# Sixteen experts in pairs: four 32-column tiles of plain fp32 in place of three split passes

## Chip, cores and metric

The kernel runs on one core of one Trainium2 chip. The metric is device time in microseconds (us) of one execution; a kernel's time is the median of its runs. The engines are named as the profile names them: PE (TensorE), PEld (its weight loads), DVE (VectorE), ACT (ScalarE), POOL (GpSimd) and SP (SyncE, which here only issues DMAs).

## What is computed

A chain of two hybrid layers (mixers and a dense FFN) is followed by a second block: an mLSTM and Fourier mixer, then a hierarchical mixture of experts. Both kernels do everything up to the router alike; the change is in the mixture. There are 256 tokens of width 1024, 4 groups of 4 experts, 2 experts chosen per token, both inside the one group that the token picked, and a hidden width of 512 per expert. All weights are fp32.

```python
g_sel = jnp.argmax(g_logits, axis=-1)                       # one group of 4
top_v, top_i = lax.top_k(e_sel, TOP_K)                      # 2 experts inside that group
w_top = jax.nn.softmax(top_v, axis=-1) * p_sel
expert_id = g_sel[..., None] * EXPERTS_PER_GROUP + top_i
combine = jnp.sum(jax.nn.one_hot(expert_id, N_EXPERTS) * w_top[..., None], axis=-2)
for e in range(N_EXPERTS):
    a = jax.nn.silu(h @ lp['w_gate'][e]) * (h @ lp['w_up'][e])
    y = y + combine[..., e, None] * (a @ lp['w_down'][e])
```

The weights of the experts are 16 x 3 x 2 MiB = 96 MiB, and each byte is read once by both kernels.

## The kernel before

**Routing** (`route`, L1211 to L1266). The router's logits stand in PSUM, tokens on partitions. A few dozen small DVE instructions rank them, and each token gets a slot, its rank among the tokens of its *group* (matmuls L1226 and L1228, `slot` L1231). `comb` holds a token's weights for the 16 experts. `over` says whether a group has more than its 128 slots.

**Gather** (`gather`, L1268). A one-hot matrix `oh` (token x slot) is built by DVE, and 32 matmuls (L1281) multiply it with the token matrix to give `xg`, the slots' inputs with the width on partitions. Two groups are gathered at a time, 256 columns per matmul. `h2h` and `h2l` are the high and the low part of the tokens; the matmuls are of type fp32r, which takes fewer bits of an operand than fp32, so a number is kept as a high part and the rest.

**One expert** (`expert_gate`, `expert_up`, `expert_split`, `expert_out`). 128 slots are the columns of the stationary operand. Each weight tile of 1 MiB is loaded into `raw`, then `split` (L189 to L192) makes two fp32r tiles of it: ACT casts to `whi` (L191), DVE subtracts to `wlo` (L192). `mm3` (L241 to L247) then runs three passes, high x high, high x low and low x high, 512 columns each. That makes 24 matmuls for gate, 24 for up and 24 for down, 72 per expert and 1152 for 16 experts. Between up and down stand 4 transposes (L1328). Four experts of a group accumulate in the same two PSUM banks, so the output is moved back to token order once per group (`combine`, 8 matmuls L1354).

**Order.** `moe` (L1361) writes the instructions so that the next expert's gate runs ahead of this expert's transposes, and up ahead of down. Each engine's queue then runs in order.

**Weight buffers.** `raw` (L194) hands out whatever is free: four tiles of a pool from earlier stages, two of `wx`, and at first places that other tensors take later. A load into a buffer waits until DVE has subtracted the last tile in it.

**End** (`finish` L1437, then L1420 and L1421). The result is normalised, added to the input and stored. Every engine then loads `over` (L1420) and branches (L1421) past a body that redoes slots beyond 128; it does not run with these inputs, before or after.

```python
for ps in range(3):                                   # L243, mm3
    for (wh, wl), (xh, xl) in terms:
        w, x = ((wh, xh), (wh, xl), (wl, xh))[ps]
        self.nc.tensor.matmul(out, w, x, ...)         # L247
```

For a later step one place of the first block matters as well: L522 to L529, where attention output is accumulated in fp32 with 64 columns of stationary, a head with an even number into PSUM partitions 0 to 63 and an odd one into 64 to 127. The loop over heads is outside, that over two blocks of keys inside.

Of the kernel before, what the change touches and what calls it, by code (L numbers as in the profile page):

```python
# [17 lines left out]
P = 128  # L18
D = 1024
NEG = -1e30  # L20
SPREAD = (0, 2, 4, 6, 1, 3, 5, 7)
# [121 lines left out]
class Build:  # L143
    def __init__(self, ctx, tc, ins, out, offs, dbg=None):
        self.tc, self.nc, self.ins, self.out, self.dbg = tc, tc.nc, ins, out, dbg or {}
        self.offs, self.at = offs, {}
        pool = lambda name, bufs, **k: ctx.enter_context(tc.tile_pool(name=name, bufs=bufs, **k))
        self.const = pool("const", 1, side="right")
        self.wraw = pool("wraw", 3)
        self.psum = pool("psum", 1, space=bass.MemoryType.PSUM)  # L150
        self.pool = pool
        self.pending = None
        self.wx, self.wy, self.nraw = None, None, 0
# [40 lines left out]
    def raw(self, shape):  # L194
        n, self.nraw = self.nraw, self.nraw + 1
        if self.wx:
            i = n % 10 if n < 20 else (n - 20) % 6
            if i == 8:
                return self.big("raw", shape[1:])
            if i >= 6:  # L200
                return self.act.tile(shape, F32, tag=("xgh", "xgl", None, "yo")[i - 6], name="raw", bufs=1 if i == 9 else 2)
            if i >= 4:
                return self.wx.tile(shape, F32, tag="raw", name="raw")
        else:
            i = n % 4
        if self.wy and i == 3:
            return self.wy.tile(shape, F32, tag="raw", name="raw")
# [1003 lines left out]
    def route(self):  # L1211
# [9 lines left out]
        rank = self.ranks(v[:, 0:2], 2, "g")  # L1221
        asg = tmp.tile([P, 2, 4], FR, tag="asg", name="asg", bufs=1)
        nc.vector.tensor_scalar(asg, rank, 0.0, None, op0=OP.is_equal)
        own = asg.bitcast(F32)
        ps = self.bank()
        nc.tensor.matmul(ps[:, 0:8], self.striu, asg.rearrange("p j g -> p (j g)"), start=True, stop=False,  # L1226
                         skip_group_check=True)
        nc.tensor.matmul(ps[:, 4:8], self.onesr, asg[:, 0], start=False, stop=True, skip_group_check=True)  # L1228
        self.slot = keep.tile([P, 2, 4, 4], F32, tag="slot", name="slot")[:, :, :, 0]
        nc.vector.tensor_scalar(self.slot, own, -1000.0, 1000.0, op0=OP.mult, op1=OP.add)  # L1230
        self.slotted = tt(self.slot, self.slot, ps[:, 0:8].rearrange("p (j g) -> p j g", j=2), op=OP.add)  # L1231
        for j in range(2):
            nc.tensor.matmul(ps[:, 8:12], self.onesr, asg[:, j], start=j == 0, stop=j == 1, skip_group_check=True)
# [7 lines left out]
        rank = self.ranks(ve, 8, "e")  # L1241
# [19 lines left out]
        self.split(comb, *(self.idc[:, :, o:o + 16].rearrange("p j (g i) -> p j g i", g=4) for o in (P, P + 16)))  # L1261
        self.over = keep.tile([P, 5], mybir.dt.int32, tag="over", name="over")
        mxc = small("mxc", 1)
        nc.vector.tensor_reduce(mxc, ps[:, 8:12], AX.X, OP.max)
        nc.vector.tensor_scalar(self.over[:, 0:4], ps[:, 8:12], 128.0, None, op0=OP.is_gt)
        nc.vector.tensor_scalar(self.over[:, 4:5], mxc, 128.0, None, op0=OP.is_gt)  # L1266

    def gather(self, p, slot):  # L1268
        nc = self.nc
        oh = self.act.tile([P, 2, 2, P], FR, tag="oh", name="oh", bufs=2)  # L1270
        for j in range(2):
            nc.vector.tensor_tensor(oh[:, j], self.p("iota")[:, None, :].to_broadcast([P, 2, P]),
                                    slot[:, j, 2 * p:2 * p + 2, None].to_broadcast([P, 2, P]), op=OP.is_equal)
        X = self.hilo("xg", 8, 256, bufs=2)
        yield oh, X
        for q in range(4):
            ps = self.bank()
            for k in range(2):
                f = slice((2 * q + k) * P, (2 * q + k + 1) * P)
                for i, (j, s) in enumerate(((0, 0), (1, 0), (0, 1), (1, 1))):  # L1280
                    nc.tensor.matmul(ps[:, k * 256:(k + 1) * 256], self.H2[s][:, j, f],  # L1281
                                     oh[:, j].rearrange("p n s -> p (n s)"), start=i == 0, stop=i == 3)
            t = self.act.tile([P, 2, 256], F32, tag="xgt", name="xgt", bufs=2)
            for k in range(2):
                m = 2 * q + k
                nc.scalar.activation(t[:, k, :], ps[:, k * 256:(k + 1) * 256], AF.Identity, bias=self.cols[:, 2, m:m + 1],
                                     scale=self.cols[:, 1, m:m + 1])
            self.split(t, X[0][:, 2 * q:2 * q + 2], X[1][:, 2 * q:2 * q + 2])
            yield

    def select(self, g, oh):
        nc = self.nc
        ps = self.bank()
        for j in range(2):
            nc.tensor.matmul(ps[:, j * 160:(j + 1) * 160], oh[:, j, g % 2, :], self.idc[:, j, :], start=True, stop=True)
        v = ps[:, 0:320].rearrange("p (j s) -> p j s", j=2)
        oT = self.act.tile([P, 2, P], FR, tag="oT", name="oT", bufs=2)
        nc.scalar.copy(oT, v[:, :, 0:P])
        cw = self.act.tile([P, 4], F32, tag="cw", name="cw", bufs=2)
        for i in range(4):  # L1300
            e = 4 * g + i
            nc.vector.tensor_reduce(cw[:, i:i + 1], v[:, :, P + e:P + 32:16], AX.XY, OP.add)
        return oT, cw

    def expert_in(self, name, e, X):
        w = self.ins[name][e].rearrange("q p (k c) -> p q k c", k=4)
        n = slice(e // 4 % 2 * P, (e // 4 % 2 + 1) * P)
# [7 lines left out]
    def expert_gate(self, e, X):  # L1315
        ga = self.tmp.tile([P, 512], F32, tag="ga", name="ga")
        self.nc.scalar.activation(ga, self.expert_in("w_gate_2", e, X), AF.Silu)
        return ga

    def expert_up(self, e, X, ga, cw):  # L1320
        self.nc.vector.scalar_tensor_tensor(ga, self.expert_in("w_up_2", e, X), cw[:, e % 4:e % 4 + 1], ga,
                                            op0=OP.mult, op1=OP.mult)

    def expert_split(self, ga):
        nc = self.nc
        ps = self.bank()
        for m in range(4):
            nc.tensor.transpose(ps[:, m * P:(m + 1) * P], ga[:, m * P:(m + 1) * P], self.c("ident"))  # L1328
        A = self.hilo("ah", 4, P, bufs=2)
        self.split(ps.rearrange("p (m s) -> p m s", m=4), *A)  # L1330
        return A

    def expert_out(self, e, A, acc):
        w = self.ins["w_down_2"][e].rearrange("q p (k c) -> p q k c", k=2)
        for q in range(2):
            W = self.weights(w[:, q], 2, 1024, -2 if e else -4)
            for hf in range(2):
                self.mm3(acc[hf], [((A[0][:, 2 * q + k, :], A[1][:, 2 * q + k, :]),
# [236 lines left out]
```

## Time and profile before

| | us |
|---|---|
| runs | 1139.29, 1140.35, 1140.89 (median 1140.35) |
| profiled execution | 1136.58 |
| its span in the profile | 1134.7 |
| PE busy | 1073.8 (95%) |
| DVE busy | 894.6 (79%) |
| ACT busy | 643.5 (57%) |
| POOL busy | 130.2 (11%) |
| read from memory | 246.01 MB, 218 GB/s over the span |

The span runs from the first to the last instruction of the profiled execution; 1.9 us lie around it. Times of a row are from the start of the span. Matmuls overlap: a row of a group gives for each matmul the time from its start to its modelled end (some 0.4 us for 512 columns), while the next one starts earlier, and the chain of waits shows the step from one start to the next. The granted clock is 1.00 where PE has its full 2.4 GHz and 0.50 at 1.2 GHz.

### The profile page before, as it was taken

What the parts mean: (1) busy time and instruction counts of PE and PEld (TensorE: products, weight loads), DVE (VectorE), ACT (ScalarE), POOL (GpSimd) and SP (SyncE); (2) the same over time, 40 slices, a digit from 0 to 9 for tenths busy, and PEclk for the clock granted to TensorE, in tenths of its full rate; (3) what the DMA queues carried; (4) which work ended last, traced back from release to release, by engine and by line L of the source; (5) the groups of instructions that cost most, each with busy time, mean ns of one, the idle gap of its engine ahead of it and who ended that gap; (6) DMA issues with size and microseconds to landing.
All of it is one profiled execution on the core that took longest, in us unless ns stands there. A gap on an engine that the chain in (4) does not pass through costs nothing.

```text
span 1134.7 us, 18470 instructions
## 1 busy us (share of the span) xinstructions
PE 1073.8 (95%) x7384; PEld 974.0 (86%) x7384; DVE 894.6 (79%) x1448; ACT 643.5 (57%) x937; POOL 130.2 (11%) x139
## 2 busy tenths in 40 slices
PE   7997999999999989899999989899899999999995
PEld 6896999999998978899999988877788888878783
DVE  6897678888777977856877778775599888998976
ACT  5635554344455364635554345743687778777763
POOL 3190010000020930310000022000000000000001
PEclk9998999999999989989999999899899999999998
DMA  8634347776754244555667750320678689989871
GB/s 283 232 112 167 131 152 275 247 254 242 268 187 149 103 158 154 213 189 210 236 237 283 294 207 24 144 75 12 265 274 339 259 323 344 350 345 371 302 299 41
DMA packets 41390, 248.34 MB, mean 219 GB/s; under 512 B 4560, under 2 KB 6992, under 8 KB 15312
## 3 DMA queue, kind: packets, MB, share of 16 engines
q1 hardware_dynamic: 41296, 247.08, 59.0%
q8 instruction: 60, 0.98, 0.3%
q14 instruction: 34, 0.28, 0.1%
HBM read 246.01 MB, written 1.05 MB: 218 GB/s over the span
## 4 chain that ended last, share of the span: by engine, by line
PE 46%; DVE 4%; ACT 2%; issue 1%; POOL 1%; POOLq 0%; DVEq 0%; ACTq 0%
PE mm L247 23%; PE acc L247 14%; DVE wlo L192 1%; ACT whi L191 1%; PE mm L1354 1%; PE mm L1281 1%; PE mm L733 1%; PE mm L1328 1%; PE acc L922 1%; PE mm L805 0%; POOL ssq L285 0%; PE mm L1063 0%; PE mm L1064 0%; DVE Mt L757 0%; PE mm L1129 0%
## 5 line engine op out<-in xcount | busy, mean ns | idle before, releaser
L191 ACT CAST whi<-raw 128x1024 fp32r<-128x1024 f32 (+2 forms) x375 | 406.0, 1124 | 262.2 <-PE mm L247 124.7
L192 DVE TENSOR_TENSOR wlo<-raw,whi 128x1024 fp32r<-128x1024 f32 (+2 forms) x375 | 484.2, 1326 | 80.5 <-ACT whi L191 79.4
L247 PE MATMUL mm<-hfh,whi 128*128 128x256 f32 x672 | 91.5, 278 | 0.1
L247 PE MATMUL mm<-hfl,whi 128*128 128x256 f32 x672 | 90.4, 277 | 0.0
L247 PE MATMUL mm<-hfh,wlo 128*128 128x256 f32 x672 | 90.1, 277 | 0.0
L285 POOL TENSOR_TENSOR ssq<-ssq,sqt 128x256 f32<-128x256 f32 x40 | 38.2, 957 | 430.1 <-ACT sqt L277 428.8
L247 PEld LDWEIGHTS mm<-hfh,whi 128*128 128x128 f32 x672 | 83.2, 188 | 0.4 <-ACT whi L191 0.4
L247 PEld LDWEIGHTS mm<-hfl,whi 128*128 128x128 f32 x672 | 82.7, 188 | 0.0
L247 PEld LDWEIGHTS mm<-hfh,wlo 128*128 128x128 f32 x672 | 82.7, 188 | 0.0
L247 PE MATMUL acc<-ffh,whi 128*128 128x256 f32 x352 | 72.0, 285 | 0.0
L247 PE MATMUL mm<-whi,xgh 128*128 128x512 f32 x256 | 71.7, 399 | 0.4 <-ACT xgh L191 0.3
L247 PE MATMUL acc<-ffh,wlo 128*128 128x256 f32 x352 | 71.0, 283 | 0.0
L247 PE MATMUL acc<-ffl,whi 128*128 128x256 f32 x352 | 70.7, 282 | 0.0
L247 PE MATMUL mm<-wlo,xgh 128*128 128x512 f32 x256 | 70.4, 395 | 0.0
L247 PE MATMUL mm<-whi,xgl 128*128 128x512 f32 x256 | 70.0, 395 | 0.0
L696 DVE CUSTOM_DVE_ANT_0 araw<-araw,arow 128x1024 f32<-128x1024 f32 x48 | 58.5, 1231 | 0.0
L247 PEld LDWEIGHTS mm<-wlo,xgh 128*128 128x128 f32 x256 | 47.9, 187 | 11.9 <-DVE wlo L192 0.3
L247 PEld LDWEIGHTS mm<-whi,xgl 128*128 128x128 f32 x256 | 48.0, 187 | 11.7
L247 PEld LDWEIGHTS mm<-whi,xgh 128*128 128x128 f32 x256 | 46.8, 188 | 11.7 <-ACT xgh L191 1.2
L247 PEld LDWEIGHTS acc<-ffh,whi 128*128 128x128 f32 x352 | 55.0, 192 | 0.2
L247 PEld LDWEIGHTS acc<-ffl,whi 128*128 128x128 f32 x352 | 54.8, 191 | 0.0
L247 PEld LDWEIGHTS acc<-ffh,wlo 128*128 128x128 f32 x352 | 54.8, 191 | 0.0
(489 smaller groups left out, 2034.8 us busy)
## 6 DMA issues: line engine op xcount, KB each, us to landing
raw<-in_w_gate_dram SPq DMA_DIRECT2D x54, 1024.0 KB, 5.4
raw<-in_w_up_dram SPq DMA_DIRECT2D x54, 1024.0 KB, 5.2
raw<-in_w_down_dram SPq DMA_DIRECT2D x54, 1024.0 KB, 4.9
raw<-in_w_in_dram SPq DMA_DIRECT2D x29, 1024.0 KB, 4.9
araw<-in_w_adaT_dram SPq DMA_DIRECT2D x48, 512.0 KB, 5.0
raw<-in_w_out_dram SPq DMA_DIRECT2D x12, 1024.0 KB, 4.8
x<-in_xT_dram SPq DMA_DIRECT2D x4, 256.0 KB, 5.5
raw<-in_w_in_dram SPq DMA_DIRECT2D x4, 256.0 KB, 5.6
```

Source lines behind the costliest of these rows:

```text
L191: nc.scalar.copy(hi, src)
L192: nc.vector.tensor_tensor(lo, src, hi.bitcast(F32), op=OP.subtract)
L247: self.nc.tensor.matmul(out, w, x, start=start and i == 0, stop=stop and i == n - 1, **kw)
L285: nc.gpsimd.tensor_tensor(self.ssq, self.ssq, sq, op=OP.add)
L696: nc.vector.tensor_tensor_reduce(out, raw, rows[n], 1.0, 0.0, OP.mult, OP.add, self.mod[:, t, n:n + 1])
L733: nc.tensor.matmul(ps[0:100, :], self.weff[:, (c + 4) % 8, :], src, start=c == 0, stop=c == 7)
L922: nc.tensor.matmul(psx[m][:, 0:258], a, b[:, k, :], start=k == 0 and i == 0, stop=k == 7 and i == 2)
L1281: nc.tensor.matmul(ps[:, k * 256:(k + 1) * 256], self.H2[s][:, j, f], oh[:, j].rearrange("p n s -> p (n s)"), start=i == 0, stop=i == 3)
L1328: nc.tensor.transpose(ps[:, m * P:(m + 1) * P], ga[:, m * P:(m + 1) * P], self.c("ident"))
L1354: nc.tensor.matmul(ps, oT[:, j, :], Y[:, s, hf, :], start=s == 0, stop=s == 1)
```

## The change

Experts p and p+8 form a pair, and there are 8 pairs. A pair has 128 slots too, but they belong to experts now: four columns of 32 slots. Column 1 is expert p+8, columns 2 and 3 are expert p, and column 0 is assigned by count: to p+8 if it has more than 32 tokens, else to p. `side[p]`, an integer made by DVE in `route`, is loaded into a PE register (`sides`, L1341), and the weight tile holds both experts' weights next to each other, so the register picks the half that the matmul of column 0 reads.

For each weight slice `quads` (L1344 to L1347) issues four matmuls, each with 32 columns of stationary, writing to its own 32 PSUM partitions, and reading 512 columns of its own expert's weights. They are plain fp32 on the weights as loaded: no `split`, no high and low. Per pair gate has 32 matmuls in 8 quads, up the same, and down, in two halves, the same; 192 quads in all.

What follows from that: a gather for every pair (L1312; 32 matmuls of 128 columns, moved out of PSUM by ACT L1319 and DVE L1316 in turn), a select and 4 transposes (L1370) for every pair, and a combine (8 matmuls, L1391) for every pair. The host lays the weights out anew, 4 tiles of 1 MiB for each of gate, up and down of a pair. The weight buffers are a ring of 16 tiles (3 of the old pool, 13 new ones). Routing gets longer (`room`, `past`, `put`, `full`, `late`, `side`, `pairs`), and three rounds for slots beyond the columns stand at the end instead of one, each behind a load and a branch (L1445, L1446).

```diff
+RING = (6, 7, 11, 8, 1, 4, 2, 5, 0, 3, 9, 10, 12)
     def raw(self, shape):
         n, self.nraw = self.nraw, self.nraw + 1
-        if self.wx:
-            i = n % 10 if n < 20 else (n - 20) % 6
...
+        if self.ring:
+            i = n % (3 + len(self.ring))
+            if i >= 3:
+                return self.act.tile(shape, F32, tag=f"ring{self.ring[i - 3]}", name="raw")
...
-        rank = self.ranks(v[:, 0:2], 2, "g")
+        rank = self.ranks(v, 10, "r")
...
+        nc.vector.tensor_scalar(self.side, ps[:, 40:48], 32.0, None, op0=OP.is_gt)
...
+    def pair(self, name, p, q):
+        w = self.raw([P, 2, 2, 512])
+        self.nc.sync.dma_start(w, self.ins[name][p, q].rearrange("p (e k c) -> p e k c", e=2, k=2))
+        return w
+
+    def sides(self, p):
+        v = self.nc.values_load(self.side[0:1, p:p + 1], engines=(mybir.EngineType.PE,), min_val=0, max_val=1)
+        return [bass.ds(v, 1), slice(1, 2), slice(0, 1), slice(0, 1)]
+
+    def quads(self, out, x, w, side, start, stop):
+        for t in range(4):
+            r = slice(32 * t, 32 * t + 32)
+            self.nc.tensor.matmul(out[r], x[:, r], w[:, side[t]].rearrange("p e c -> p (e c)"), start=start, stop=stop)
+
+    def pair_in(self, name, p, X, side):
         ps = self.bank()
-        for q in range(2):
-            W = self.weights(w[:, q], 4, 512, -2 if e else -4, self.held if q else ())
-            self.mm3(ps, [((X[0][:, 4 * q + k, n], X[1][:, 4 * q + k, n]), (W[0][:, k, :], W[1][:, k, :]))
-                          for k in range(4)], start=q == 0, stop=q == 1)
+        for q in range(4):
+            w = self.pair(name, p, q)
+            for k in range(2):
+                self.quads(ps, X[:, 2 * q + k], w[:, :, k, :], side, q == 0 and k == 0, q == 3 and k == 1)
         return ps
...
+        for r in range(3):
+            rv = nc.values_load(self.over[0:1, 3, r:r + 1])
+            with self.tc.If(rv > 0):
```

**PE, an expert and a pair.** In the rows, `whi` and `wlo` are the two parts of a weight tile, `xgh` and `xgl` those of the gathered slots, `ga` the gated product, `raw` a weight tile as loaded, `xg` the gathered slots in fp32. Before, the end of a gate, the transposes of the expert ahead, and an up:

```order
L247 MATMUL mm<-whi,xgh 128x512 x4
L247 MATMUL mm<-wlo,xgh 128x512 x4
L247 MATMUL mm<-whi,xgl 128x512 x4
L1328 MATMUL mm<-cst_160,ga 128x128 x4
L247 MATMUL mm<-whi,xgh 128x512 x4
L247 MATMUL mm<-wlo,xgh 128x512 x4
L247 MATMUL mm<-whi,xgl 128x512 x4
```

Now, the first gate, from the gather's last matmuls on:

```order
L1312 MATMUL mm<-oh,h2l 128x128 x3
L1347 ISA
L1347 MATMUL mm<-raw,xg 32x512
L1312 MATMUL mm<-oh,h2h 128x128 x2
L1312 MATMUL mm<-oh,h2l 128x128 x2
L1347 MATMUL mm<-raw,xg 32x512 x3
L1347 ISA
L1347 MATMUL mm<-raw,xg 32x512 x4
L1347 ISA
L1347 MATMUL mm<-raw,xg 32x512 x4
```

Each quad stands behind one register instruction (ISA), and is a row of its own. The gather's last four matmuls stand inside the first quad, behind its first matmul; such broken quads come 8 times. In all the queue changes between 32-column matmuls and matmuls of the full width 115 times.

**SP, the loads around the start of the mixture.** `in_w_out_dram` is the last weight of the mixer. Before:

```order
L229 DMA raw<-in_w_out_dram 128x2048 x4
L234 DMA raw<-in_w_up_dram 128x2048
L234 DMA raw<-in_w_gate_dram 128x2048 x2
L234 DMA raw<-in_w_up_dram 128x2048
L234 DMA raw<-in_w_gate_dram 128x2048 x3
L234 DMA raw<-in_w_down_dram 128x2048 x2
L234 DMA raw<-in_w_up_dram 128x2048 x2
```

Now:

```order
L1337 DMA raw<-in_w_gate_dram 128x2048 x4
L1337 DMA raw<-in_w_up_dram 128x2048 x4
L1337 DMA raw<-in_w_gate_dram 128x2048 x4
L1337 DMA raw<-in_w_up_dram 128x2048 x4
L1337 DMA raw<-in_w_down_dram 128x2048 x4
```

The loads now come in the order in which PE reads them, the first 16 into 16 buffers; load 17 waits until PE has read load 1.

**DVE, routing.** `slot` is what the one-hot matrix `oh` needs, `h2l` is the low part of the tokens. Before, from `slot` to `h2l`:

```order
L1231 TENSOR_TENSOR slot<-slot,mm 128x8
L1244 TENSOR_SCALAR top<-rank 128x32
L1245 TENSOR_SCALAR second<-rank 128x32
L1272 TENSOR_TENSOR oh<-cst_5015,slot 128x256
...
L1272 TENSOR_TENSOR oh<-cst_5015,slot 128x256
L1161 SCALAR_TENSOR_TENSOR h2l<-x_8185,rs_8845,h2h 128x512
```

Now:

```order
L1246 SCALAR_TENSOR_TENSOR put<-put,sel 128x32
L1285 TENSOR_TENSOR room<-mm,room 128x16
L1247 SCALAR_TENSOR_TENSOR slot<-put 128x16
L1272 TENSOR_TENSOR w_8947<-w_8947,psel 128x8
L1286 TENSOR_TENSOR most<-room 128x8
L1295 TENSOR_TENSOR oh<-cst_5015,slot 128x256
...
L1281 TENSOR_TENSOR pairs<-comb 128x16
L1156 SCALAR_TENSOR_TENSOR h2l<-x_8185,rs_8845,h2h 128x512 x2
```

Between the matmuls that count the tokens and `slot` stand some 20 small instructions now, 2 before; between the first `oh` and `h2l` 13 in place of 9.

## Rows read from the trace of the kernel before

**Rows 1.** Page, part 1: each engine's busy time, share of the span, instructions.
```profile
PE 1073.8 (95%) x7384; PEld 974.0 (86%) x7384; DVE 894.6 (79%) x1448; ACT 643.5 (57%) x937; POOL 130.2 (11%) x139
```
**Rows 2.** Chain of waits that ended last, in the mixture: start us, us, what.
```profile
830.19 2.61 PE mm L247 x10
...
847.35 0.44 PE mm L1328 x4
847.79 5.59 PE mm L247 x24
...
1109.36 10.07 PE acc L247 x42
1119.43 1.43 PE mm L1354 x4
```
**Rows 3.** Window table: stretch, busy us of each engine, granted clock, DMA share, GB/s.
```profile
814.00:824.00 10.00, 7.33 (x31) 6.73 (x32) 6.28 (x36) 7.28 (x18) 0.98 (x1) 0.50 0.80 318
830.00:1104.00 274.00, 273.74 (x1229) 220.83 (x1230) 243.87 (x259) 209.17 (x250) 0.00 (x0) 1.00 0.85 326
804.00:812.00 8.00, 8.00 (x43) 6.37 (x41) 3.83 (x7) 4.39 (x13) 1.10 (x2) 1.00 0.96 389
1020.00:1040.00 20.00, 20.00 (x89) 16.13 (x89) 17.82 (x17) 14.93 (x17) 0.00 (x0) 1.00 0.95 365
```
**Rows 4.** Timeline of PE around plain fp32 matmuls of 512 columns (L892).
```profile
696.35 1.02 PE L892 MATMUL mm<-par,cst 128*128 128x512 f32 x2
697.21 0.38 PE L805 MATMUL mm<-vt,kw 128*128 128x129 f32 x2
```
**Rows 5.** Timeline of PE around two places with 64-column fp32 matmuls.
```profile
424.68 0.50 PE L247 MATMUL mm<-xnh,wlo 128*128 128x256 f32 x2
425.11 1.09 PE L527 MATMUL acc<-pT,vt 128*64 128x128 f32 x14
426.13 0.39 PE L247 MATMUL mm<-xnh,wlo 128*128 128x256 f32 x1
...
85.67 0.66 PE L538 MATMUL mm<-wsT,ones 128*64 128x128 f32 x8
```
**Rows 6.** Durations of such a line (ns, min/median/max).
```profile
L538 PE MATMUL mm<-wsT,ones x16: 272/273/323, 85.7 to 402.9; 128*64 128x128 f32 x16
```
**Rows 7.** Chain of waits: small matmuls of the mixture.
```profile
905.27 0.94 PE mm L1281 x8
...
1082.64 1.79 PE mm L1176 x16
```
**Rows 8.** Line L1420, the load of the test's value into a register, by engine's queue.
```profile
L1420 DVEq TENSOR_LOAD <-over x1: 753/753/753, 1127.9 to 1127.9; - x1
L1420 SPq TENSOR_LOAD <-over x1: 482/482/482, 1129.7 to 1129.7; - x1
```
**Rows 9.** Line L1421, the branch, and what stands behind it (EVENT_SEMAPHORE), by queue.
```profile
L1421 SPq EVENT_SEMAPHORE  x9: 17/17/17, 1132.7 to 1133.3; - x9
...
L1421 DVEq EVENT_SEMAPHORE  x2: 21/21/21, 1132.3 to 1132.4; - x2
...
L1421 SPq COMPARE_BRANCH  x1: 45/45/45, 1130.2 to 1130.2; - x1
```
**Rows 10.** Timeline of DVE in routing.
```profile
821.14 0.28 DVE L1205 TENSOR_TENSOR gt<-lt 128x128 f32<-128x128 f32 x1
821.34 0.18 DVE L1208 TENSOR_REDUCE rank<-gt 128x8 f32<-128x32 f32 x1
821.44 0.28 DVE L1206 TENSOR_TENSOR ge<-ge,cst 128x128 f32<-128x128 f32 x1
...
822.54 0.17 DVE L1231 TENSOR_TENSOR slot<-slot,mm 128x8 f32<-128x8 f32 x1
...
824.99 0.75 DVE L1161 SCALAR_TENSOR_TENSOR h2l<-x,rs,h2h 128x512 fp32r<-128x512 f32 x1
```
**Rows 11.** Timeline of SP: three of the mixture's first loads, four stand ahead of them.
```profile
802.87 1.28 SPq L234 DMA_DIRECT2D raw<-in_w_gate_dram  x3
```

More of the change, by code (lines that the diff above doesn't have):

```diff
@@ new lines, in route @@
+        self.slot = keep.tile([P, 2, 8], F32, tag="slot", name="slot")
+        put = small("put", 2, 2, 8)
+        for h, b in enumerate((64.0, 32.0)):
+            nc.vector.tensor_scalar(put[:, :, h], before[:, :, h], b, -2 * b, op0=OP.is_ge, op1=OP.mult)
+            nc.vector.scalar_tensor_tensor(put[:, :, h], before[:, :, h], b, put[:, :, h], op0=OP.add, op1=OP.add)
+        full = small("full", 2, 2, 8)
+        nc.vector.tensor_scalar(full, past, 0.0, 1000.0, op0=OP.is_ge, op1=OP.mult)
@@ L1266, in route @@
-        nc.vector.tensor_scalar(self.over[:, 4:5], mxc, 128.0, None, op0=OP.is_gt)
-    def gather(self, p, slot):
-        nc = self.nc
[L1270 to L1276, printed above, removed]
+        pairs = small("pairs", 2, 2, 4)
@@ new lines, in route @@
+        tt(pairs, comb[:, :, 0:2], comb[:, :, 2:4], op=OP.add)
+        self.split(pairs, *(self.idc[:, :, o:o + 8].rearrange("p j (g i) -> p j g i", g=2) for o in (P, P + 8)))
+        self.over = keep.tile([P, 4, 8], mybir.dt.int32, tag="over", name="over")
+        most, big = small("most", 8), small("big", 1)
+        tt(room, ps[:, 32:48].rearrange("p (h e) -> p h e", h=2), room, op=OP.subtract)
+        tt(most, room[:, 0], room[:, 1], op=OP.max)
+        nc.vector.tensor_reduce(big, most, AX.X, OP.max)
@@ L1283, in gather @@
[L1283 to L1291, printed above, removed]
+                    nc.tensor.matmul(ps[:, k * P:(k + 1) * P], self.H2[s][:, j, m * P:(m + 1) * P],
+                                     oh[:, j], start=i == 0, stop=i == 3)
@@ L1342, in group_out, with pair_out @@
-    def group_out(self, acc):
+        nc.scalar.copy(A, ps.rearrange("p (m s) -> p m s", m=4))
+        return A
+    def pair_out(self, p, A, side):
         Y = self.act.tile([P, 2, 2, 512], FR, tag="yo", name="yo")
         for hf in range(2):
-            self.split(acc[hf], Y[:, 0, hf, :], Y[:, 1, hf, :])
+            acc = self.bank("acc", 4)
+            for q in range(2):
+                w = self.pair("w_down_2", p, 2 * hf + q)
+                for k in range(2):
+                    self.quads(acc, A[:, 2 * q + k], w[:, :, k, :], side, q == 0 and k == 0, q == 1 and k == 1)
+            self.split(acc, Y[:, 0, hf, :], Y[:, 1, hf, :])
@@ new lines, in moe @@
+        for r in range(3):
+            rv = nc.values_load(self.over[0:1, 3, r:r + 1])
+            with self.tc.If(rv > 0):
+                late = self.tmp.tile([P, 2, 2, 8], F32, tag="sl2", name="sl2", bufs=1)
+                nc.vector.tensor_scalar(late, self.late, -64.0 * r, None, op0=OP.add)
+                for p in range(8):
+                    rp = nc.values_load(self.over[0:1, r, p:p + 1])
+                    with self.tc.If(rp > 0):
+                        oh = self.hot(p, late)
+                        X = self.gather(oh)
+                        oT, cw = self.select(p, oh)
+                        ga = self.pair_gate(p, X, side)
+                        self.pair_up(p, X, side, ga, cw)
+                        self.combine(y, oT, self.pair_out(p, self.pair_turn(ga), side))
+                self.finish(x2, y, yg, g2)
@@ L1517, in run @@
         phb.close()
+        phw.close()
         pha.close()
         if stop != "mix":
-            self.wx, self.nraw = pool(ph3, "wx", 2), 0
+            self.ring, self.wy, self.nraw = RING, None, 0
             self.act = pool(ph3, "act3")
+            for i in range(len(RING)):
+                self.act.tile([P, 2048], F32, tag=f"ring{i}", name="place")
             self.tmp = pool(ph3, "tmp3", 2)
```

222 lines of the change are left out of this document (103 added, 119 removed).

## The prediction, made before the changed kernel was timed

> **What bounds the kernel now.** I read the page's first part, then the chain of waits, then a window table of the mixture. Part 1 gives PE 95% of the span and DVE 79% [rows 1], an average over stages. The chain shows the stage that is changed: from 830.19 to 1119.43 us it is PE alone, gate and up, transposes, down, one after another [rows 2]; in the window from 830 to 1104 PE is busy 273.74 of 274.00 us at granted clock 1.00, with DVE at 243.87 and the DMA share 0.85 [rows 3]. So in these 289.2 us PE sets the time. A group of 24 matmuls takes 5.59 us, 0.233 us each, and 1152 x 0.233 = 268.8; transposes, gathers, combines and selects make up the rest. The reader should see that splitting, however busy DVE is, is covered: to delete it saves nothing by itself.
>
> The sum goes against the profiled execution, 1136.58 us (span 1134.7, 1.9 around it), which is 3.8 us under the median of the runs.
>
> **PE: 1152 fp32r matmuls go, 192 quads come.** A plain fp32 matmul has two records, one per pass; two records of 512 columns start at 696.35 and the next work at 697.21, so it takes 0.86 us, 0.43 a pass [rows 4]. The price of a quad hangs on whether its four matmuls run at once. The nearest rows have two column tiles of 64: 8 records in 0.66 us and 14 in 1.09 us [rows 5], where one record lasts 0.272 [rows 6]. The 14 are seven calls, and by the loops their order is one head's call in the lower tile, two in the upper, two lower, two upper: 6 records for the lower tile and 8 for the upper. Eight steps of 0.109 us plus the first step's 0.05 and the last record's tail give 7 x 0.109 + 0.05 + 0.27 = 1.08: the time of the longer tile alone. So the two tiles run side by side, though a tile's own records stand four in a row. I take the same for four tiles: 0.86 us per quad. The ends are 0.86 and, if none run together, 3.44; what I hold possible in between are the rivals below.
>
> The Trainium skill's page "TensorE: Matmul & The Clock Gate", section "Part 3: Packing small matmuls — row/col tiling", says that matmuls start and end strictly in program order. Here that rule would make a quad 1.72 us and the kernel some 165 us longer than my sum; the 14 records speak against it, and it is rival D.
>
> The terms of the new stretch:
> - 192 quads x 0.86 = 165.1.
> - 8 broken quads: a lone first matmul costs a full 0.86 and the other three another, so 8 x 0.86 = 6.9.
> - Gathers of 7 more pairs, 7 x 32 matmuls of 128 columns. Matmuls of the full width with few columns take 0.11 (4 in 0.44 [rows 2], 16 in 1.79 [rows 7]); half of a 256-column one (8 in 0.94 [rows 7]) would be 0.06. I take 0.11, as a weight load comes with each: 24.6.
> - Combines 64 x 0.233 = 14.9, transposes 32 x 0.11 = 3.5, selects 16 x 0.11 = 1.8, the row of L1176 1.8 as before.
> - Changes of tile shape. Around the 14 records [rows 5] I find four delays. The full-width matmul ahead starts at 424.90 (two with a record of 0.28 fill 0.50) and needs 0.12, yet the first tile starts at 425.11: 0.09. The first step is 0.05 longer. The last start is 425.11 + 0.05 + 7 x 0.109 = 425.92, yet the next matmul starts at 426.13, not 0.11 later: 0.10. That one lasts 0.39 in place of 0.28: 0.11. Together 0.35 us a round trip. 115 changes are 57 round trips: 19.9. The low end is nothing, if the next weights load meanwhile.
> - 8 loads of `side` into a register: 0.48 us each, as SP's queue shows one [rows 8], plus two register instructions, at most 4.6, at least nothing, as PE has queued work; I take 2.4. The 192 register instructions ahead of the quads: the nearest row is a branch of 45 ns on a queue [rows 9], so at most 9; the queue runs ahead by 0.86 us per quad, so nothing.
> - The clock is at 0.50 while PE waits for the routing [rows 3]: 1.5 for the first quads, between 0 and 3.
>
> The sum is 242.4 us against 289.2: **46.8 less**. Per pair that is 30.3 us.
>
> **What leaves the other engines.** The 192 casts and subtractions go; nothing waited for them, so no gain. ACT and DVE take on the evacuation of seven gathers, 8 small instructions per pair on two engines that lose 24 large ones each: covered by 30 us of PE per pair.
>
> **The start is later.** `slot` is ready at 822.54 now [rows 10]. The ranks of ten rows rather than two cost 5 x 0.1 more (128 elements take a step of 0.20, 32 elements 0.10 [rows 10]); some 20 small instructions at about 0.10 stand ahead of `slot`, of which two stood there before. Against that, the half of the gather's evacuation on DVE and the split of `xg` that is gone bring the first quad forward. The low part `h2l`, now behind 13 small instructions, comes at 827 to 828 instead of 824 to 825.7 and the gather waits for it. I put the first quad at 831.9 where the first matmul stood at 830.19: **+1.7**, between -1 and +4.
>
> **The tail is longer.** Two more tests stand on each queue, one after the other. SP's load takes 0.48, its branch 0.05, and from the branch at 1130.2 to what stands behind it at 1132.7 it is 2.5; DVE's load starts at 1127.9 and takes 0.75, and what stands behind its branch is at 1132.3, together 4.4 [rows 8, 9]. Two more are 2 x 3.0 to 2 x 4.4: I take **+7**, between 0 (if the later jumps are cheap) and 9.
>
> **The loads.** 96 MiB as 96 loads of 1 MiB, now in the order of use. A busy stretch had 389 GB/s at share 0.96 (2.70 us per MiB), the best 20 us in the mixture 365 (2.87) [rows 3]. Before, the first seven loads were out by 804.2 [rows 11]; the first of them wait for the same buffers now, so I count seven landed at 812. Nine more at 2.70 fill the ring of 16 at 836, when PE has begun to free it; the 80 left take 216 us, to 1052, while PE works to 832 + 242 = 1074. So the stream is covered by 22 us; it would bind from 3.0 us per MiB on (350 GB/s). What is late next, if PE were faster, is this stream.
>
> Together: -46.8 + 1.7 + 7 = -38.1, so 1098.5 for the profiled execution and, 3.8 higher, **1102 us** on the scale of the medians.
>
> **Rivals.**
> - **B, cheaper PE.** Gathers at 0.06 (-11) and tile changes hidden (-20) leave 211 us of PE, to 1043; then the loads bind, at 2.70 us to 1052 and 3 for the last work, so 19 us are gained on 1074: 1083. Where they don't bind it is all 31: 1071. For it: queues on PE run ahead of the array. Against it: the rows of 0.11 and of the tile changes, measured here.
> - **E, the loads bind.** The mean of the mixture, 326 GB/s [rows 3], is 3.22 us per MiB: 80 x 3.22 = 257, to 1093, and 3 for the last: +22, 1124. For it: that mean. Against it: those loads waited for DVE to free buffers.
> - **C, four tiles overlap in part.** Four streams of columns have to be read where the rows show two. By the rows a quad then lies between 0.86 and D's 1.72; a quarter of the way is 1.08, and 192 x 0.22 = +42 gives 1144, about as before. Against it: with two tiles the rows show no loss at all. The Trainium skill's table in the same section has three column tiles at 2.38 times the speed of one; an efficiency of 0.79 would, as an estimate from that page, make a quad 1.09 us and the time about the same 1144; no run here shows it yet.
> - **D, the order of the matmuls decides.** If a matmul cannot start before the one ahead of it in the queue, the second pass of column 0 holds column 1, and so on; each quad then takes four steps of 0.43, 1.72 us: +165, **1267 us, slower**. The same price follows if the matmul with the register's address does not run beside the others. It decides from a quad of 1.06 us on (38.1 / 192 = 0.20 above 0.86). For it: no row here has a register as an address, nor four tiles. Against it: the 14 records.
>
> **How the numbers follow.** A measurement of this kernel can tell about 0.2%, 2.3 us, from no change. The forecast, with E inside it, 1085 to 1128: 0.67, and 1102 is its likeliest value. B, 1067 to 1085: 0.12. C, 1128 to 1155: 0.09, half of it still faster. D, around 1267: 0.12. The range 1067 to 1149 takes in the forecast, B and most of C and leaves D out, which is a little over one in ten. Faster: 0.67 + 0.12 + 0.04 = 0.83; within 0.2%: 0.02; slower: 0.15.
>
> **What would show it.** The line of `quads`: four starts within some ns and 0.86 us between quads is right, 1.08 is C, starts 0.43 apart is D. In the chain, the mixture should stay PE alone; DMA as a releaser of PE in its second half means E. The gather's 32 matmuls should take 3.5 us per pair, PE's stretch 242 us, and the span should end some 22 us after the last quad (15.3 before, from 1119.43 to 1134.7, and 7). A first quad after 836, or PE idle between pairs, would prove me wrong as well.

## The result, and the profile after

The changed kernel takes 1109.31 us (median of four runs, 1105.07 to 1113.50) against 1139.82 us for the kernel before: a ratio of 0.9741, with a 95% interval of 0.9692 to 0.9790. The forecast was 1102 us, within 1067 to 1149, faster. The direction held, and so did the price of a quad, on which the sum rests; the gain is 30 us where 38 were forecast.

The profiled execution took 1113.50 us, with a span of 1111.7; it is the slowest of the four. The page's first part, beside [rows 1]:

```profile
PE 1034.0 (93%) x7968; PEld 839.7 (76%) x7968; DVE 682.0 (61%) x1282; ACT 455.4 (41%) x737; POOL 129.7 (12%) x139
```

DVE lost 213 us of work and ACT 188, and that is not where the 30 us came from: PE is still the engine that sets the end. The chain of waits in the mixture answers to [rows 2] (start us, us, what):

```profile
840.24 1.85 PE mm L1347 x2
842.09 1.05 PE mm L1312 x4
843.13 7.69 PE mm L1347 x62
850.83 0.38 PE mm L1327 x2
851.20 7.00 PE mm L1347 x64
858.20 0.61 PE mm L1312 x4
858.84 0.47 ACT xg L1319
859.35 0.79 PE mm L1312 x5
860.13 0.40 DVE xg L1316
...
888.53 0.98 PE acc L1347 x2
889.51 0.59 PE mm L1312 x4
890.10 0.99 PE acc L1347 x8
891.09 0.59 PE mm L1312 x4
891.68 5.71 PE acc L1347 x51
...
921.49 4.42 PE acc L1347 x36
925.91 0.42 PE mm L1391
926.33 2.26 PE acc L1347 x17
...
1089.84 0.59 ACT yo L192
1090.48 1.25 PE mm L1391 x3
```

The row 851.20 answers the main question. 64 records are 8 quads of 8 records, and they take 7.00 us, so four matmuls of 512 columns run in the time of one, 0.86 to 0.875 us. Three things in these rows were not in the forecast. At 858.84 and 860.13 PE waits for ACT and DVE to empty a bank of the gather. The rows at 888.53 and 890.10 hold broken quads, and so do those around 925.91, where a combine matmul cuts into a quad: the 36 records ahead of it end six records into one. And the two records at 840.24 take 1.85 us, twice what they take later. The window table says why (columns as in [rows 3]; the last three numbers are the granted clock, the DMA share and GB/s):

```profile
840.00:844.00 4.00, 4.00 (x16) 1.45 (x19) 0.82 (x2) 1.74 (x2) 0.00 (x0) 0.50 0.50 205
844.00:858.00 14.00, 14.00 (x128) 3.94 (x120) 0.59 (x2) 0.86 (x2) 0.00 (x0) 0.98 0.81 314
858.00:862.00 4.00, 3.34 (x26) 2.78 (x23) 1.32 (x3) 1.64 (x4) 0.00 (x0) 0.95 1.01 422
862.00:872.00 10.00, 10.00 (x39) 3.97 (x43) 1.47 (x4) 0.46 (x1) 0.00 (x0) 0.51 0.61 240
884.00:888.00 4.00, 3.28 (x27) 2.81 (x24) 1.32 (x3) 1.64 (x4) 0.00 (x0) 1.00 1.01 422
888.00:898.00 10.00, 10.00 (x83) 3.70 (x86) 2.16 (x5) 1.16 (x3) 0.00 (x0) 1.00 0.94 351
1000.00:1040.00 40.00, 40.00 (x318) 16.22 (x314) 8.29 (x17) 6.31 (x13) 0.00 (x0) 1.00 1.01 421
```

From 840 to 844 and again from 862 to 872 PE has the lower of its two clock levels, 1.2 GHz. Before the second stretch stands the one with the waits for the evacuation, 858 to 862, where PE was idle for 0.66 of 4 us; PE is then busy all the time at 0.51 and does less than half the work, 39 records against 83 in the 10 us from 888. The same waits come again from 884 to 888, with 0.72 us of idle time, and there the clock stays at 1.00 behind them. So these waits alone do not decide whether the clock falls; what does stays open. From 1000 to 1040 the DMA share is 1.01 at 421 GB/s, while PE is busy 40.00 of 40: both are full.

Where routing begins, and when the one-hot matrix is ready (timeline of DVE), beside [rows 10]:

```profile
826.24 0.38 DVE L1212 SCALAR_TENSOR_TENSOR lt<-mm,rs,brow 128x20 f32<-128x20 f32 x2 [2.60 <-PE mm L1124]
...
832.17 0.42 DVE L1295 TENSOR_TENSOR oh<-cst,slot 128x256 fp32r<-128x256 f32 x1
```

The first of these rows stands at 819.96 in the profile before. Everything ahead of it is the same work in both kernels, and the same row lies anywhere from 818.2 to 826.2 us in the thirteen profiles with the changed kernel's code ahead of it, mostly with how long the clock was at half in the stages ahead (33 us in the profile with 818.2, 50 in that with 826.2). So below, times are also counted **from this row to the end of the span**, which leaves that out: 314.8 us before, 285.5 after.

### The profile page after: what moved, and what is told of

Read it like the earlier page. It is cut to its first block, busy times and chain, and to the rows that moved or that the text cites. A ratio compares the mean times of both kernels' runs of the same rounds, so it can differ in the third digit from the quotient of the medians.

```text
span 1111.7 us, 19437 instructions
## 1 busy us (share of the span) xinstructions
PE 1034.0 (93%) x7968; PEld 839.7 (76%) x7968; DVE 682.0 (61%) x1282; ACT 455.4 (41%) x737; POOL 129.7 (12%) x139
## 4 chain that ended last, share of the span: by engine, by line
PE 44%; DVE 4%; ACT 2%; issue 1%; POOL 1%; POOLq 0%; DVEq 0%; ACTq 0%
PE mm L1347 11%; PE mm L242 8%; PE acc L242 6%; PE acc L1347 6%; PE mm L1312 3%; PE mm L1391 2%; DVE wlo L193 1%; PE mm L728 1%; PE acc L917 1%; PE mm L800 0%; PE mm L1370 0%; POOL ssq L280 0%; PE mm L1058 0%; PE mm L1059 0%; PE mm L780 0%
## 5 line engine op out<-in xcount | busy, mean ns | idle before, releaser
L192 ACT CAST whi<-raw 128x2048 fp32r<-128x2048 f32 (+1 forms) x171 | 213.2, 1272 | 219.8 <-PE mm L242 95.7
L193 DVE TENSOR_TENSOR wlo<-raw,whi 128x2048 fp32r<-128x2048 f32 (+1 forms) x171 | 257.9, 1521 | 62.7 <-ACT whi L192 61.9
L1347 PE MATMUL mm<-raw,xg 128*32 128x512 f32 (+1 forms) x1024 | 128.8, 609 | 0.0
L1347 PEld LDWEIGHTS mm<-raw,xg 128*32 128x32 f32 x1024 | 32.1, 111 | 67.0 <-issue 65.0
L1347 PE MATMUL acc<-raw,ah 128*32 128x512 f32 (+1 forms) x512 | 66.1, 596 | 0.0
L1316 DVE TENSOR_SCALAR xg<-mm,cols 128x128 f32<-128x128 f32 x32 | 12.4, 407 | 63.4 <-PE mm L1312 63.4
L1312 PEld LDWEIGHTS mm<-oh,h2h 128*128 128x128 f32 x128 | 21.5, 211 | 38.2 <-issue 23.6
L1319 ACT ACTIVATE xg<-mm,cols 128x128 f32<-128x128 f32 x32 | 14.6, 458 | 70.7 <-PE mm L1312 70.6
```

Of the source, the lines that this page charges most:

```text
L192: nc.scalar.copy(hi, src)
L193: nc.vector.tensor_tensor(lo, src, hi.bitcast(F32), op=OP.subtract)
L1312: nc.tensor.matmul(ps[:, k * P:(k + 1) * P], self.H2[s][:, j, m * P:(m + 1) * P], oh[:, j], start=i == 0, stop=i == 3)
L1316: nc.vector.tensor_scalar(X[:, m, :], o, self.cols[:, 1, m:m + 1], self.cols[:, 2, m:m + 1], op0=OP.mult, op1=OP.add)
L1319: nc.scalar.activation(X[:, m, :], o, AF.Identity, bias=self.cols[:, 2, m:m + 1], scale=self.cols[:, 1, m:m + 1])
L1347: self.nc.tensor.matmul(out[r], x[:, r], w[:, side[t]].rearrange("p e c -> p (e c)"), start=start, stop=stop)
```

## The experiments

Every time is the median, and every ratio is to the kernel before on the same chip; e1 to e4 ran on one chip, e5 to e8 on a second, e9 to e11 on a third and e12 on a fourth, so across these groups the ratios are compared. "Router to end" is the time just described, from the one profiled execution of each.

| run | us | ratio to before (95%) | router to end, us |
|---|---|---|---|
| before | 1139.82 | | 314.8 |
| the change | 1109.31 | 0.9741 (0.9692 to 0.9790) | 285.5 |
| e1 the change again | 1110.35 | 0.9754 (0.9725 to 0.9783) | 286.4 |
| e2 no register | 1111.28 | 0.9742 (0.9711 to 0.9773) | 286.7 |
| e3 tests nested | 1105.57 | 0.9686 (0.9650 to 0.9722) | 286.5 |
| e4 gather in four banks | 1094.29 | 0.9609 (0.9583 to 0.9635) | 270.9 |
| e5 = e4 and e3 | 1083.76 | 0.9516 (0.9486 to 0.9546) | 262.0 |
| e6 = e5, whole stages | 1068.58 | 0.9384 (0.9355 to 0.9412) | 247.6 |
| e7 = e6, half the quads | 1056.90 | 0.9286 (0.9247 to 0.9324) | 234.6 |
| e8 = e6, clock kept up | 1066.24 | 0.9371 (0.9336 to 0.9406) | 242.0 |
| e9 = e6, gather by twos, 14 buffers | 1066.12 | 0.9375 (0.9345 to 0.9404) | 244.3 |
| e10 = e9 and e8 | 1064.88 | 0.9356 (0.9326 to 0.9386) | 242.0 |
| e11 = e8 again | 1065.24 | 0.9364 (0.9334 to 0.9394) | 242.0 |
| e12 = e6, 14 buffers | 1069.99 | 0.9394 (0.9372 to 0.9417) | 246.6 |

**e1, the change again.**

> The changed kernel, unaltered, as the measure for the others. Theory A (its time differs from run to run with the granted clock of the stages ahead of the mixture): median 1105 to 1113, the first router row of DVE between 820 and 827 us; the stretch from the first quad to the last combine 246 to 251 us each time, and the 10 us at half clock around 862 us come again, because PE waits for the gather's evacuation just before. Theory B (that cold stretch is chance): it is missing, and the stretch is some 5 us shorter.

Theory A. The cold stretch is there again, 10.2 us long from 857.8, right behind the same waits, and the router's row lies at 822.2. The stretch from the first quad (836.1) to the start of the last combine matmul (1087.7) is 251.6 us, a little over the range; counted the same way the change has 251.4.

**e2, no register.**

```diff
     def sides(self, p):
-        v = self.nc.values_load(self.side[0:1, p:p + 1], engines=(mybir.EngineType.PE,), min_val=0, max_val=1)
-        return [bass.ds(v, 1), slice(1, 2), slice(0, 1), slice(0, 1)]
+        return [slice(0, 1), slice(1, 2), slice(0, 1), slice(0, 1)]
```

> Column 0 always takes expert p: no register, no load of side, no register instruction ahead of a quad (so the slots of pairs with more than 32 tokens at p+8 are computed with the wrong weights). Theory A (the queue runs ahead of the array, the register costs next to nothing): 0 to 2.4 us less than the changed kernel, all of it around the eight loads; a full quad stays 0.86 to 0.88 us. Theory B (an address in a register holds the matmul back): quads get shorter, 192 times some 0.015 to 0.05, 3 to 10 us less.

The time is that of e1, 0.9742 to 0.9754, and eight quads take 7.00 us without a register as with one (row 851.20 above). The chain in e2, then the register instructions of the changed kernel (ns, min/median/max):

```profile
849.81 7.00 PE mm L1346 x64
```
```profile
L1347 PEldq FUSED_REGOPS  x192: 51/55/65, 838.9 to 1085.5; - x192
```

192 instructions of 55 ns are 10.6 us of PE's sequencer, and none of it shows in the time: theory A, at its lower end. The 2.4 us that the forecast set aside for the loads of `side` were not seen; router to end is 0.3 us longer than in e1.

**e3, one test on the path.**

```diff
-        for r in range(3):
+        def round_(r):
             rv = nc.values_load(self.over[0:1, 3, r:r + 1])
             with self.tc.If(rv > 0):
...
-                self.finish(x2, y, yg, g2)
+                if r < 2:
+                    round_(r + 1)
+                if r == 0:
+                    self.finish(x2, y, yg, g2)
+        round_(0)
```

> The second and third overflow test stand inside the body of the first, so that one load and one branch are on the path. Theory A (each test that is passed costs 2.5 to 4 us of load and jump): the time from the last combine matmul to the end of the span falls from 21 to about 15.5 us, 5 to 6 us less in all. Theory B (the longer tail comes from something else, the cold clock or the longer stores): less than 1.5 us less.

The last matmul in the chain ends at 1096.8 here and the span at 1108.8: 12.0 us, where the change has 1091.7 to 1111.7, 20.0. So the two tests cost 8 us, 4 each, more than I expected. From the modelled end of the last matmul to the end of the span it is 19.8 to 21.5 us in the four profiles with three tests in a row (the change, e1, e2, e4) and 11.8 to 12.5 in the nine with nested tests. SP's branches and what stands behind the last of them, in the change and then in e3:

```profile
L1446 SPq EVENT_SEMAPHORE  x27: 17/17/17, 1102.4 to 1110.4; - x27
...
L1446 SPq COMPARE_BRANCH  x3: 45/45/50, 1099.6 to 1107.1; - x3
```
```profile
L1446 SPq EVENT_SEMAPHORE  x9: 17/17/17, 1106.9 to 1107.5; - x9
...
L1446 SPq COMPARE_BRANCH  x1: 45/45/45, 1104.2 to 1104.2; - x1
```

SP goes through three branches from 1099.6 to 1107.1, 3.75 us each, and arrives at 1110.4. The median of the whole is only 4.8 us under e1, though, and router to end is the same: the profiled execution had two more cold stretches in the mixture, 10.2 us each from 883.5 and 917.6, behind the second and the third place where the gather waits, where the change and e1 stayed at full clock. Its runs lie between 1095.8 and 1112.9. With the second gather's waits gone the gain shows whole: e5 is 10.5 us under e4 (ratios 0.9516 and 0.9609).

**e4, the gather in four banks.**

```diff
-        for q in range(2):
-            ps = self.bank()
-            for k in range(4):
-                m = 4 * q + k
...
+        pss = [self.bank("acc" if b % 2 else "mm") for b in range(4)]
+        for m in range(8):
+            o = pss[m % 4][:, m // 4 * P:(m // 4 + 1) * P]
```

> The gather's eight groups of four matmuls go round four PSUM banks in place of filling one bank after another; everything else is as in the changed kernel, but the order on PE changes: 95 changes of tile shape in place of 113, one broken quad in place of fifteen. Theory A (each group waited for the evacuation of the group ahead in the same bank, and the waits put gather pieces between quads): 4 us of waits for ACT and DVE go, 6 us of broken quads, 9 round trips of 0.3 us, and 4 us of cold clock behind the waits, in all 12 to 17 us less than the changed kernel. Theory B (the waits are hidden or move to another place): less than 3 us less.

Theory A: 16 us less than e1, and the clock, once up behind the first quads, does not fall again inside the mixture. The chain around the second gather, and the window that was cold:

```profile
846.92 7.00 PE mm L1344 x64
853.93 0.59 PE mm L1311 x4
854.52 0.45 PE acc L1311 x4
854.97 0.45 PE mm L1311 x4
...
857.65 0.23 PE mm L1324 x2
857.88 7.00 PE mm L1344 x64
```
```profile
862.00:872.00 10.00, 10.00 (x96) 3.05 (x88) 0.00 (x0) 1.14 (x2) 0.00 (x0) 1.00 1.02 425
```

The gather takes 3.72 us with no wait in it, where the change went from 858.20 to 863.12 and had eight matmuls left. The window from 862 to 872 has 96 matmul records at clock 1.00, against 39 at 0.51 in the change. Not all waits are gone: at 891.32, 902.25 and later places the chain still goes through an evacuation for 0.4 to 0.5 us. The 16 us are not split among waits, broken quads, round trips and clock by a run of their own. A gather writes a bank while the group ahead in the same bank is being moved out; the kernel makes it wait for that, and the order on PE, which is fixed ahead, filled those waits with quads and broke them.

**e5, both.**

> The gather in four banks and the nested tests together. Theory A (the two gains lie in different places and add): the tail from the last combine matmul to the end of the span 12 us in place of 21.5, the mixture as with the four banks alone: 1085 to 1087 us. Theory B (the shorter tail is an effect of that run's order): above 1091 us.

1083.76 us: theory A, and a little more. The tail is 12.7 us from the last matmul's end.

**e6, whole stages.** The edges put every PE instruction of a stage behind the last one of the stage ahead.

```diff
+    def stage(self):
+        return self.tc.issue_after(self.tail.ins)
...
-            A = self.pair_turn(ga[p])
+            with self.stage():
+                A = self.pair_turn(ga[p])
```

> As e5, and PE's queue is held to whole stages by ordering edges (gate, then transposes with the combine of the pair ahead, up, gather with select, down): 37 changes of tile shape in place of 95, no broken quad. Theory A (a round trip costs some 0.3 us of PE): 29 round trips less, 7 to 10 us less than e5, about 1077 us. Theory B (the loads bind by now, 2.5 us each and 30 us per pair): PE waits for loads in the second half and the time falls by less than 4 us.

15.2 us less than e5, more than A had it. One pair, as it now repeats:

```profile
898.64 7.00 PE acc L1344 x64
905.64 6.87 PE mm L1344 x64
912.51 0.59 PE mm L1367 x4
913.10 1.86 PE mm L1388 x8
914.96 7.00 PE mm L1344 x64
921.96 0.59 PE mm L1311 x4
922.56 0.45 PE acc L1311 x4
```

These rows price the change of tile shape. Eight quads take 6.87 us with quads behind them and 7.00 with a full-width matmul behind: 0.13 on the way out. The first four full-width matmuls take 0.59 in place of 0.45: 0.14 on the way in. A round trip is 0.27 us; 29 of them less are 7.8. Most of the rest stands in e5's chain and not in e6's: four waits for an evacuation (1.8 us), two more waits for the split of the last outputs (1.2), one of 0.8 for `ga`, a quad broken by a combine matmul (0.9) and 0.4 of issue.

**e7, half the quads.** `for k in range(2)` in `pair_in` and `pair_out` becomes `k = 0` alone; the loads stay.

> As e6, but every second quad is left out, so half of each product is missing; all loads stay. Theory A (the loads take 2.5 us each whatever PE does, so they are the floor under this design): the last load lands at about 1039 us, the span ends some 17 us behind it, 1056; 18 to 22 us less than e6, not the 83 us that 96 quads take. Theory B (PE's own reading of the weights slows the loads down): loads come faster, below 2.35 us each, and the span ends before 1045.

Theory A: the last load landed at 1039.0, and the span ended at 1054.1. 96 quads fewer, 83 us of PE work, are worth 12 us, since PE now waits for loads. The window table and the waits of PE (us in total, times, longest):

```profile
920.00:960.00 40.00, 31.29 (x192) 14.34 (x188) 9.32 (x18) 5.68 (x11) 0.00 (x0) 0.83 1.01 422
```
```profile
PE mm L1344 <- DMA raw<-in_w_gate_dram: 16.4, 14, 1.5
...
PE acc L1344 <- DMA raw<-in_w_down_dram: 7.9, 8, 1.4
```

422 GB/s are 2.49 us per MiB, the same as with all the quads (421), so PE's reading takes nothing from the loads that can be seen here. I expected 18 to 22 us under e6 and got 12: e6 itself came out 8 us lower than I thought.

**e8 and e11, the clock kept up.** 6 matmuls of 512 columns ahead of the count matmuls, 8 behind them.

```diff
+        spare = self.bank("acc", 4)
+        dummy = lambda n: [nc.tensor.matmul(spare, self.onesr, self.H2[0][:, i % 2, 0:512], start=True, stop=True,
+                                            skip_group_check=True) for i in range(n)]
+        dummy(6)
         nc.tensor.matmul(ps[:, 0:32], self.striu, ...)
...
+        dummy(8)
```

> As e6, with 14 matmuls of 512 columns, whose output nobody reads, in the two places of the routing where PE waits for DVE. Theory A (the half clock in the first gather and the first quads comes from PE's idle time in the routing): the clock is at 1.00 before the first quad, the first gather takes 4 us in place of 7, and the time falls by 3 to 6 us. Theory B (the clock rises no sooner): the same time, or up to 1 us more, as the count matmuls wait behind the extra ones.

> e8 once more, beside e9 and e10 on the same chip, as its runs were spread over 12 us. Theory A: 1062 to 1068 us, the half clock ends before the first quad. Theory B (that was chance): the half clock lasts into the first quads again and the time is e6's, 1068 us.

In both profiles the full clock is back before the first quad. The half clock around the router lasts 10.2 to 13.7 us in the three profiles with the extra matmuls (e8, e10, e11) and 17.1 to 23.9 in the ten changed kernels without; e9 is the one without them where it too ends before the first quad. The first gather takes 3.8 us in e8 where e6 has 7.1. The windows of e8, up to its first quad at 829.2 and from there:

```profile
824.00:829.00 5.00, 5.00 (x36) 4.71 (x34) 4.30 (x22) 1.73 (x5) 0.00 (x0) 0.81 1.02 429
829.00:842.00 13.00, 13.00 (x121) 4.09 (x123) 1.00 (x3) 2.44 (x4) 0.00 (x0) 1.00 1.01 419
```

Router to end is 242.0 us in both, 5.6 less than e6, as theory A has it. Of the whole time only 2 to 3 us can be seen, less than the 3 to 6 of theory A, and the intervals of e6 and e8 overlap; the stages ahead of the router vary by more than that.

**e9 and e10, the gather by twos.** One gather for two pairs, 256 columns per matmul, 4 gathers; two ring buffers less, for the wider `xg`.

> As e6, but the gather is made for two pairs at a time, 256 columns per matmul as in the kernel before, in 4 gathers in place of 8 (the ring has 14 buffers in place of 16 for it). Theory A (a gather matmul costs 0.11 us for 128 columns and 0.118 for 256, and the loads are the floor): PE loses 14.8 us of work and would end at 1039, the loads stop it at about 1043, and the time is some 10 us under e6, 1057 to 1060 us. Theory B (PE is still the bound, or the smaller ring starves it): either the whole 14.8 us come, below 1055, or less than 5 us.

> As e9, with the 14 extra matmuls of e8 in the routing. Theory A (the loads are the floor by now): the first quad comes 3 us sooner, and the time stays that of e9 within 1.5 us, 1056 to 1060 us; PE waits for loads in the last third. Theory B (PE is still the bound): 3 to 5 us under e9.

e9 is no 10 us under e6: a miss. The ratios, 0.9375 and 0.9384, can't be told apart, and router to end is 3.3 us less. That is the part of theory B by which the smaller ring starves it (less than 5 us). What theory A said of the floor is there, though; PE now waits for loads (us in total, times, longest):

```profile
PE mm L1346 <- DMA raw<-in_w_gate_dram: 4.8, 9, 0.7
...
PE acc L1346 <- DMA raw<-in_w_down_dram: 3.4, 6, 0.6
```

But the stream itself was later: the last load landed 225.9 us after the router's row, against 221.9 in e6 and 219.5 in e7. e10, with the clock kept up, is within 1.3 us of e9, as expected of a kernel that the loads bind, but at 1064.9 us and not the 1056 to 1060 expected. Router to end fell by 2.3 us, and so did the landing of the last load (223.7 us after the router's row): the gap behind the 14th load is 4.3 us there, 7.0 in e9, so here too the end follows the loads.

**e12, fourteen buffers.** `RING` of 11 in place of 13, on e6.

> As e6, with 14 weight buffers in place of 16 and nothing else, to tell apart what held e9 back. Theory A (with two buffers less the stream of loads stops sooner, before PE frees the first one, and never makes it up): after the 14th load there is a gap of 5 to 7 us between landings where e6 has one of under 5 after its 16th, the last load lands some 4 us later, counted from the first router row of DVE, than e6's 222 us; the time itself stays within 3 us of e6, as PE is the bound here. Theory B (the later loads of e9 came from its wider gather): the last load lands within 1.5 us of e6's.

Theory A, with a gap and a delay a little larger than expected. By the landing times the 14th and the 15th load are 7.7 us apart here, where e6 has 4.7 us behind its 16th, and the last load lands 227.1 us after the router's row, 5.2 later than in e6. That gap is 3.0 us of the delay; a second one, which the expectation did not name, lies ahead of it: 5.9 us between the 6th and the 7th landing, where e6 has 2.5. The time is that of e6. So e9 paid with the ring for what it gained on PE. A gather by twos with 16 buffers was not tried.

## Why the prediction was right, and what it missed

**PE's stretch** was to fall from 289.2 to 242.4 us; it is 250.2, from 840.24 to 1090.48.

- *A quad, 0.86.* Right: 6.87 / 8 = 0.859 (e6), as the call in [rows 4]. From the two tiles of 64 columns in [rows 5] it could not be known that four of 32 run side by side; the step from two to four was a bet, and it held.
- *Rival D, the order of the matmuls.* Ruled out by the same rows: 1.72 us would have made the 64 records last 13.8. The two records at 840.24 run alone ahead of the gather's matmuls and are one call, so I take a quad to be queued as two records for column 0, two for column 1 and so on. In the trace, at full clock, the records start in groups of four within 10 to 20 ns, one of each group being that of column 0, the one with the register, and the groups are 0.43 us apart. I take each group to hold one record of each column. The timeline of PE in two narrow windows (each row is two groups, the one in hand and the next):

```profile
844.65 1.03 PE L1347 MATMUL mm<-raw,xg 128*32 128x512 f32 x8
```
```profile
845.08 1.03 PE L1347 MATMUL mm<-raw,xg 128*32 128x512 f32 x8
```

So the first record of column 3 starts 0.43 us ahead of the second one of column 2, which stands before it in that order. The Trainium skill's page "TensorE: Matmul & The Clock Gate", section "Part 3: Packing small matmuls — row/col tiling", states that matmuls start and end strictly in program order; with the queue read as above, this trace shows otherwise for the starts of matmuls in different column tiles. D's second ground, the register, is out by e2.

- *Rival C, 1.08.* Ruled out as well. The 2.38 that the Trainium skill has for three column tiles, in the same section, stands against 4 x 0.86 / 0.86 = 4.0 for four tiles here; the measurement decides for this kernel.
- *Rival B, cheaper PE.* Out by the two terms that it doubted: a gather matmul takes 0.112 us and not 0.06, and a change of tile shape 0.27 and not nothing (below).
- *Broken quads, 6.9.* The price was right, the count in the text ahead of the prediction was not: pieces of a gather break 15 quads, in 8 places, and a combine matmul breaks one more (925.91 above). Where two follow each other, the first's last three matmuls and the second's lone one run together (the row of 0.99 above), so each place costs one quad time: nine places, 7.7 us, 0.9 more than in the sum.
- *Gathers, 24.6.* Right: 3.72 us for 32 matmuls in e6, of which 0.14 is the change of tile shape, so 0.112 each.
- *Tile changes, 19.9.* Too high: 57 round trips of 0.27 are 15.4. The Trainium skill's page "TensorEngine Tiling (Array Packing)", section "Key Properties", says that a change of tiling mode drains the engine; the rows of e6 agree, at 0.13 and 0.14 us.
- *Register loads, 2.4.* Nothing (e2).
- *Not in the sum: waits.* This is the step that failed. The chain has 2.8 us of ACT and 1.2 of DVE for the gather's evacuation, 2.4 of ACT for the split of the last outputs and 0.8 of DVE in the last pair, 7.2 in all. I had put the evacuation down as covered by 30 us of PE per pair. An evacuation that is small in sum can still stand in PE's way, if PE's next instruction writes the same bank. I had also named PE idle between pairs as a sign of being wrong: it came, 2.1 us at the gathers by PE's own waits.
- *Not in the sum: the clock.* The 10 us at half clock behind those waits cost 5 us. The first quads cost 2.1 by the clock, where I had 1.5.

242.4 + 7.2 + 5.1 + 0.6 + 0.9 - 4.5 - 2.4 = 249.3, and 0.9 us are left without a name. It is luck that the miss is not larger: the two terms that were too high, 6.9 us together, hide half of the 12.3 that stood in no term. The waits at the second gather and the cold stretch behind them came together, and in e4 went together, but the link is not strict: two like waits in the change were followed by no fall of the clock.

**The start** was to be 1.7 us later; counted from the router's row it is 3.8 (14.0 to the first quad, 10.2 before). 3.1 of it are the longer chain of small DVE instructions, 5.9 us to the one-hot matrix in place of 2.8; I had counted the instructions rightly, but hoped to win some back in the gather, which at half clock takes as long as before. The forecast named a first quad after 836 as a sign of being wrong, and in the profile it comes at 840.2; 6.3 us of that lie ahead of the router, in stages that the change does not touch, and without them it is 834.

**The tail** was to be 7 us longer; from the start of the last combine matmuls it is 5.9 (21.2 against 15.3), and e3 shows that the tests are the cause.

**The loads** were covered, as forecast, by more: the last one landed at 1058.4, some 28 us before its quads ran. No DMA stands among those that PE waited for. Where nothing held the stream it ran at 421 GB/s; with its waits for buffers the 80 loads behind the first 16 took 2.69 us each, as the sum had it. e7 and e9 show that this stream is next: rival E was right about what comes after PE, not about this kernel.

Together: -39.0 for PE, +3.8 and +5.9 make -29.3, which is what the profiles differ by from the router to the end.

## What to carry to other kernels

When a stage is bound by one engine, count the work that this engine does, not what the others lose: by the chain, the gain here comes from 289 us of PE becoming 250, and 213 us less on DVE are not in it. What a plan of terms misses is order: waits of PE for other engines and the stretch at half clock behind them cost 12 of the 47 us that the plan promised in this stage. After such a change look at the order on the engine that binds, piece by piece: two edits to it (banks in turn, whole stages) and one to the tests gave 1068.58 us, ratio 0.9384 (0.9355 to 0.9412), 41 us under the change itself; keeping the clock up as well gave 1065 to 1066.

## What the runs showed that I had not expected

- Four fp32 matmuls in four column tiles cost as much as one of the full width, 0.859 us against 0.86: 8 quads in 6.87 us (e6), with loads landing beside them (414 GB/s from 880 to 1040).
- Less than a microsecond of PE's idle time, 0.66 us in 4, was followed by half clock, in the change for 10 us. It came in all four profiles of the kernels whose second gather waited (the change and e1 to e3), and inside the mixture in none of e4, e5, e6 or e8 to e12. But it does not follow each time: behind the third and the fourth gather, with as much idle time, the clock fell in e3 and stayed up in the change, e1 and e2.
- A test at the end that is passed cost about 4 us here, for a body that never runs.
- Two weight buffers of sixteen moved the end of a stream of 96 loads by 5 us, through two gaps near its start, of 5.9 and 7.7 us.
